# Scaling a retention read-out's rows on GpSimd, one multiplication per chunk, in a two-layer hybrid decoder trunk

## The chip, the cores and the metric

The kernel runs on one core of one Trainium2 chip. The metric is the time of one execution in microseconds on the device, the median of several runs; less is better. The profile calls the engines PE (TensorE, matmuls), PEld (its weight loads), DVE (VectorE), ACT (ScalarE), POOL (GpSimd) and SP (SyncE, which here only issues DMAs).

## The reference

Two layers over 512 positions of width 1024, in float32. Each layer normalizes x, projects it, sends the parts through three branches (an RWKV-7 recurrence, a chunked retention, a spatial gating unit), merges the three with sigmoid gates, and adds a gated MLP with a short convolution. The change touches the end of the retention branch:

```python
def retention_branch(p, cos, sin):
    ...
    y = (inner + cross).transpose(0, 2, 3, 1, 4).reshape(B, S, RET_HEADS, RET_V_DIM)
    y = y * lax.rsqrt(jnp.mean(y * y, axis=-1, keepdims=True) + EPS)
    return (y.reshape(B, S, RET_V_WIDTH) * jax.nn.silu(g)).astype(p.dtype)
...
        branches = jnp.stack([y_rw, y_ret, y_sg], axis=2)
        proj = jnp.einsum('bsgc,gcd->bsgd', branches, w_branch[l])
        gates = jax.nn.sigmoid(gate_logits.reshape(B, S, N_BRANCH, D_MODEL))
        x = x + jnp.sum(gates * proj, axis=2) @ w_out[l]
```

There are 4 heads of 128 columns, and 4 chunks of 128 positions. Each row of each head of y is divided by the root of its mean square.

## The kernel before, in words

**Matmuls and weights.** Every float32 product with weights is three matmuls (`mm3`, L153) over a high and a low half of both factors. A weight unit of 128x512 is loaded from HBM by SP into one of three raw buffers (`wr`, L123); ScalarE casts it to the high half (`sh` or `wh`, L136) and VectorE subtracts to get the low half (`sl` or `wl`, L137), after which the raw buffer may be loaded again. `unit` does this a few units ahead of the matmuls. Activations are split in the same way by `split` (L145 `hi` on ScalarE, L146 `lo` on VectorE). The products gather in PSUM accumulators: 4 of `acc`, 4 of `sm`.

**The order of the work.** The program is written in one sequence; a scheduler puts the instructions of every engine in an order, and `keep_in_program_order` pins some, the matmuls among them. Each engine then works off its own queue in that order. In the end of a layer's mixer the string `SEQ` sets the sequence: `0`, `1` and `2` are merges of one 128-column block with branch 0 (RWKV), 1 (retention) and 2 (spatial gating); `H` loads the retention's heads, `G` is a gating unit's output, and each `S` is one `ret_row`. The first `S` makes the scores, the second reads out chunks 0 and 1, the third chunks 2 and 3. `Y` is `ret_out`, which transposes the finished rows on TensorE (L964) and splits them for the merges `1`.

```python
SEQ = "0 H 0 0 0 G G S U U G S 0 G S 0 0 2 2 0 2 2 Y 2 1 2 1 2 1 2 1 1 1 1 1"
```

**The read-out.** For its two chunks `ret_row` squares the 8 head parts on ScalarE with a row sum each (L948), multiplies them from PSUM into the gate's tile on VectorE (L950, `yg`, which the profile calls `vt`), turns the sums into a mean plus epsilon (L951, `rss`), and lets GpSimd raise the 128x8 sums to the power -1/2 (L953, `rrr`). Each of the 8 parts of 128x128 is then scaled in place by its column of `rrr`, on ScalarE (L957).

**A merge** loads the gate from DRAM (L1027, `gth`), multiplies it with the accumulator on VectorE (L1028), which frees the accumulator, and adds to the running sum: on GpSimd for branch 2 (L1031), on VectorE for branch 1.

Of the kernel before, what the change touches and what calls it, by code (L numbers as in the profile page):

```python
# [10 lines left out]
AF = mybir.ActivationFunctionType  # L11
ALU = mybir.AluOpType
AX = mybir.AxisListType
ADD, SUB, MUL, POW, MAX = ALU.add, ALU.subtract, ALU.mult, ALU.pow, ALU.max
# [35 lines left out]
class Emit:  # L50
# [857 lines left out]
    def ret_row(self, read):  # L908


        nc, V, A, T, po = self.nc, self.nc.vector, self.nc.scalar, self.nc.tensor, self.tc.keep_in_program_order
        hv = [slice(0, 64), slice(64, 128)]
        X, new = [self.sm((128, 4, 128)) for _ in range(2)], [[True, True], [True, True]]
        hd = [(j, p, h) for j in range(2) for p in range(2) for h in (1, 0)]

        def mm(b, q, o, lhsT, rhs, stop=True):
            po(T.matmul(o, lhsT, rhs, start=new[b][q], stop=stop, skip_group_check=True))  # L917
            new[b][q] = False

        if read is None:  # L920
            for c in range(NC):
                for j, p, h in hd:
                    ts = slice(64 * p, 64 * p + 64)
                    mm(h, h ^ j, X[h][hv[h ^ j], c, ts], self.kF[j][hv[h], c, ts], self.qF[j][hv[h], c, ts])
            self.ret_states(0, 4)
            self.sc = [self.u((128, 8, 64), n="sc") for _ in range(2)]
            for h in range(2):
                V.tensor_tensor(self.sc[h], X[h].rearrange("q c (p t) -> q (c p) t", t=64), self.c("le64").unsqueeze(1).to_broadcast([128, 8, 64]), op=MUL)
            return
        cs = range(read, read + 2)  # L930
        for c in cs:
            for j, p, h in hd:
                i, o = 2 * j + h, h ^ j
                w = self.vt[c][hv[p], 128 * i:128 * i + 128] if p == o else self.vs[c][hv[o], j, :]
                mm(o, p, X[o][hv[p], 2 * (c - read) + j, :], self.sc[h][hv[o], 2 * c + p, :], w, c == p == 0)
        for c in cs:
            for j, p, h in hd:
                if c or p:
                    o, ts = h ^ j, slice(128 * c + 64 * p, 128 * c + 64 * p + 64)
                    q = self.qS if j else self.qF[0].rearrange("p c t -> p (c t)")  # L940
                    mm(o, p, X[o][hv[p], 2 * (c - read) + j, :], q[hv[o], ts], self.Rs[2 * c + p][hv[o], j, :])
        if read == 0:
            self.ret_states(4, 7)
        ss = self.small((128, 2, 4), "rss")
        for c in cs:
            sq, g = self.u((128, 4, 128), n="rsq"), self.yg[c]
            for i in range(4):
                A.activation(sq[:, i, :], X[i % 2 ^ i // 2][:, 2 * (c - read) + i // 2, :], AF.Square, accum_out=ss[:, c - read, i:i + 1])  # L948
            for o in range(2):
                V.tensor_tensor(self.heads(g, o), X[o][:, 2 * (c - read):2 * (c - read) + 2, :], self.heads(g, o), op=MUL)  # L950
        V.tensor_scalar(ss, ss, 4.0 / 128, 4e-6, op0=MUL, op1=ADD)  # L951
        rr = self.small((128, 2, 4), "rrr")
        nc.gpsimd.tensor_tensor(rr, ss, self.c("mhalf")[:, 0:8].rearrange("p (c i) -> p c i", i=4), op=POW)  # L953
        for c in cs:
            for i in range(4):
                o = self.yg[c][:, 128 * i:128 * i + 128]
                A.activation(o, o, AF.Copy, scale=rr[:, c - read, i:i + 1])  # L957

    def ret_out(self):
        out = []  # L960
# [344 lines left out]
```

## Time and profile before

| | |
|---|---|
| median of 3 runs | 1702.96 us (1702.8 to 1703.59) |
| profiled execution | 1703.05 us, of which the span of its instructions is 1701.3 us |
| granted TensorE clock | 0.999 |
| busy: PE, PEld, DVE, ACT, POOL | 1691.9, 1390.8, 1148.9, 766.5, 220.0 us |
| HBM | 181.92 MB read, 23.07 MB written, 120 GB/s over the span |

The read-outs lie near 388 to 408 us of the span in layer 0 and near 1234 to 1252 us in layer 1. A row of the time line reads: start, duration, engine, line, operation, output and inputs, shapes, count, and in brackets how long the engine had been idle and what ended that. A wait is put down to what came last. Idle time of an engine that nothing waits for costs nothing.

### The profile page before, as it was taken

What the parts mean: (1) busy time and instruction counts of PE and PEld (TensorE: products, weight loads), DVE (VectorE), ACT (ScalarE), POOL (GpSimd) and SP (SyncE); (2) the same over time, 40 slices, a digit from 0 to 9 for tenths busy, and PEclk for the clock granted to TensorE, in tenths of its full rate; (3) what the DMA queues carried; (4) which work ended last, traced back from release to release, by engine and by line L of the source; (5) the groups of instructions that cost most, each with busy time, mean ns of one, the idle gap of its engine ahead of it and who ended that gap; (6) DMA issues with size and microseconds to landing.
All of it is one profiled execution on the core that took longest, in us unless ns stands there. A gap on an engine that the chain in (4) does not pass through costs nothing.

```text
span 1701.3 us, 28310 instructions
## 1 busy us (share of the span) xinstructions
PE 1691.9 (99%) x10564; PEld 1390.8 (82%) x10564; DVE 1148.9 (68%) x2016; ACT 766.5 (45%) x1341; POOL 220.0 (13%) x274
## 2 busy tenths in 40 slices
PE   9999999999999999999999999999999999999998
PEld 7888877887888888888888888778888888888887
DVE  7887856567868777753358786565687788887432
ACT  7564433535445444342255634345354544444322
POOL 1122235102100000000011203341030000000010
PEclk9999999999999999999999999999999999999999
DMA  5335565446543333243332345555464444432531
GB/s 171 93 102 152 146 152 150 142 136 196 149 127 97 98 99 95 69 121 108 119 112 81 106 149 150 147 143 164 121 214 143 123 126 123 122 107 68 155 99 56
DMA packets 154409, 214.20 MB, mean 126 GB/s; under 512 B 48416, under 2 KB 57248, under 8 KB 154272
## 3 DMA queue, kind: packets, MB, share of 16 engines
q1 hardware_dynamic: 136464, 184.21, 36.6%
q10 hardware_dynamic: 12048, 19.00, 3.4%
q0 software_dynamic: 5760, 9.19, 2.6%
q8 instruction: 83, 1.36, 0.3%
q14 instruction: 54, 0.44, 0.1%
HBM read 181.92 MB, written 23.07 MB: 120 GB/s over the span
## 4 chain that ended last, share of the span: by engine, by line
PE 98%; DMA 1%; ACT 1%; DVE 0%; issue 0%; POOL 0%; SPq 0%; DVEq 0%; POOLq 0%; ACTq 0%
PE acc L153 87%; PE sm L153 4%; PE sm L649 2%; PE acc L289 1%; PE sm L563 1%; DMA wr<-wall 1%; PE sm L917 1%; PE acc L1014 0%; DMA x<-xT 0%; PE sm L900 0%; PE sm L526 0%; PE sm L525 0%; PE sm L807 0%; DVE sl L137 0%; PE sm L797 0%
## 5 line engine op out<-in xcount | busy, mean ns | idle before, releaser
L153 PE MATMUL acc<-lo,sh 128*128 128x512 f32 x1108 | 431.8, 390 | 1.1 <-DVE lo L146 0.8
L153 PE MATMUL acc<-hi,sh 128*128 128x512 f32 x1108 | 431.2, 389 | 0.0
L153 PE MATMUL acc<-hi,sl 128*128 128x512 f32 x1108 | 429.9, 389 | 0.0
L136 ACT CAST sh<-wr 128x512 fp32r<-128x512 f32 (+1 forms) x385 | 235.2, 616 | 382.4 <-PE acc L153 265.1
L137 DVE TENSOR_TENSOR sl<-wr,sh 128x512 fp32r<-128x512 f32 (+1 forms) x385 | 268.4, 700 | 143.4 <-ACT sh L136 82.0
L153 PEld LDWEIGHTS acc<-lo,sh 128*128 128x128 f32 x1108 | 207.9, 188 | 46.4 <-DVE lo L146 1.7
L153 PEld LDWEIGHTS acc<-hi,sl 128*128 128x128 f32 x1108 | 208.0, 188 | 43.5
L153 PEld LDWEIGHTS acc<-hi,sh 128*128 128x128 f32 x1108 | 208.0, 188 | 42.9 <-issue 0.2
L136 ACT CAST wh<-wr 128x512 fp32r<-128x512 f32 x194 | 120.2, 620 | 228.1 <-PE acc L153 204.7
L153 PE MATMUL acc<-lo,wh 128*128 128x512 f32 x556 | 219.5, 395 | 0.0
L153 PE MATMUL acc<-hi,wl 128*128 128x512 f32 x556 | 217.0, 390 | 0.0
L153 PE MATMUL acc<-hi,wh 128*128 128x512 f32 x556 | 216.6, 390 | 0.0
L137 DVE TENSOR_TENSOR wl<-wr,wh 128x512 fp32r<-128x512 f32 x195 | 139.1, 713 | 111.5 <-ACT wh L136 106.9
L153 PEld LDWEIGHTS acc<-lo,wh 128*128 128x128 f32 x556 | 104.3, 188 | 22.7 <-issue 0.3
L153 PEld LDWEIGHTS acc<-hi,wl 128*128 128x128 f32 x556 | 104.3, 188 | 22.6 <-issue 0.7
L153 PEld LDWEIGHTS acc<-hi,wh 128*128 128x128 f32 x556 | 104.4, 188 | 21.0
L153 PE MATMUL acc<-ah,sh 128*128 128x512 f32 x352 | 108.3, 389 | 0.0
L1081 DVE TENSOR_TENSOR fu<-acc,rsF 128x512 f32<-128x512 f32 x88 | 60.5, 690 | 70.3 <-PE acc L153 70.2
L1083 ACT ACTIVATE cv<-fu,pc 128x512 f32<-128x512 f32 x88 | 71.6, 816 | 46.9 <-DVE fu L1081 44.3
L1084 DVE SCALAR_TENSOR_TENSOR cv<-fu,pc,cv 128x511 f32<-128x511 f32 x88 | 65.5, 747 | 18.7 <-ACT cv L1083 18.7
L153 PE MATMUL acc<-wl,hi 128*128 128x512 f32 x192 | 78.0, 406 | 0.0
L153 PEld LDWEIGHTS acc<-ah,sh 128*128 128x128 f32 x352 | 66.1, 188 | 13.7
(334 smaller groups left out, 2420.9 us busy)
## 6 DMA issues: line engine op xcount, KB each, us to landing
wr<-wall SPq DMA_DIRECT2D x480, 256.0 KB, 2.7
gd<-gth ACTq DMA_DIRECT2D x48, 256.0 KB, 2.7
gth<-gd SPq DMA_DIRECT2D x48, 256.0 KB, 4.1
wr<-wdt SPq DMA_DIRECT2D x44, 256.0 KB, 2.8
wr<-wdn SPq DMA_DIRECT2D x40, 256.0 KB, 2.6
x<-xT SPq DMA_DIRECT2D x8, 256.0 KB, 4.8
tn<-ysq POOLq DMA_DIRECT2D x32, 64.0 KB, 3.3
tab<-rot ACTq DMA_DIRECT2D x8, 256.0 KB, 3.3
```

The lines of the kernel that those rows point to most:

```text
L136: self.kept((high or self.nc.scalar.copy)(hi[:, :n], raw[:, :n]))
L137: self.kept(self.nc.vector.tensor_tensor(lo[:, :n], raw[:, :n], hi[:, :n], op=SUB))
L153: i = self.nc.tensor.matmul(*x, **y, **kw)
L289: po(self.nc.tensor.matmul(pss[j], w[:, j * 128:j * 128 + 128], x, start=k == n == 0, stop=k == 7 and n == 2))
L563: i = T.matmul(pK[hv[1 - h], j, :], bk[hv[h], c, 1, :], x[hv[h], c, :], start=True, stop=True)
L649: po(T.matmul(o, l, r, start=start, stop=True, skip_group_check=True))
L917: po(T.matmul(o, lhsT, rhs, start=new[b][q], stop=stop, skip_group_check=True))
L1081: V.tensor_tensor(u, ps, self.rsF, op=MUL)
L1083: A.activation(t, u, AF.Identity, scale=self.p("cw2", j), bias=self.p("cb", j))
L1084: V.scalar_tensor_tensor(t[:, 1:], u[:, :511], self.p("cw1", j), t[:, 1:], op0=MUL, op1=ADD)
```

## The change

The 8 scalings of a read-out (4 heads in each of 2 chunks) leave ScalarE. GpSimd, which has just computed `rrr`, multiplies each chunk's whole 128x512 tile by the chunk's 4 columns of `rrr`, each repeated over the 128 columns of its head.

```diff
         nc.gpsimd.tensor_tensor(rr, ss, self.c("mhalf")[:, 0:8].rearrange("p (c i) -> p c i", i=4), op=POW)
         for c in cs:
-            for i in range(4):
-                o = self.yg[c][:, 128 * i:128 * i + 128]
-                A.activation(o, o, AF.Copy, scale=rr[:, c - read, i:i + 1])
+            o = self.yg[c].rearrange("p (i e) -> p i e", e=128)
+            nc.gpsimd.tensor_tensor(o, o, rr[:, c - read, :].unsqueeze(2).to_broadcast([128, 4, 128]), op=MUL)
```

The new multiplication is L956, and lines below it are one lower than before. GpSimd's queue in layer 0, from the first power to the first sums of the merges, before:

```order
L953 TENSOR_TENSOR rrr_4458<-rss_4442,con 128x8
L953 TENSOR_TENSOR rrr_4552<-rss_4536,con 128x8
L1031 TENSOR_TENSOR gth_4106<-gth_4106,gth_4606 128x512
L1031 TENSOR_TENSOR gth_4153<-gth_4153,gth_4629 128x512
L1031 TENSOR_TENSOR gth_4175<-gth_4175,gth_4674 128x512
```

and after, where vt_3732 and vt_3737 are the tiles of chunks 0 and 1, vt_3742 and vt_3747 those of chunks 2 and 3:

```order
L953 TENSOR_TENSOR rrr_4458<-rss_4442,con 128x8
L956 TENSOR_TENSOR vt_3732<-vt_3732,rrr_4458 128x512
L956 TENSOR_TENSOR vt_3737<-vt_3737,rrr_4458 128x512
L953 TENSOR_TENSOR rrr_4546<-rss_4530,con 128x8
L956 TENSOR_TENSOR vt_3742<-vt_3742,rrr_4546 128x512
L956 TENSOR_TENSOR vt_3747<-vt_3747,rrr_4546 128x512
L1030 TENSOR_TENSOR gth_4106<-gth_4106,gth_4594 128x512
```

Each power now has two multiplications behind it, and the sums of the merges stand behind the second pair. ScalarE's queue at the second read-out of layer 0, from its last squares to the first split of the transposed rows, before:

```order
L948 ACTIVATE rsq_4544,rss_4536<-sm_4502 128x128 x2
L136 CAST sh_4678<-wr_4631 128x512
L957 ACTIVATE vt_3742<-vt_3742,rrr_4552 128x128 x4
L957 ACTIVATE vt_3747<-vt_3747,rrr_4552 128x128 x4
L136 CAST sh_4701<-wr_4654 128x512
L136 CAST sh_4760<-wr_4676 128x512
L136 CAST sh_4783<-wr_4699 128x512
L136 CAST sh_4810<-wr_4758 128x512
L136 CAST sh_4833<-wr_4781 128x512
L136 CAST sh_4860<-wr_4808 128x512
L145 CAST hi_4725<-sm_4720 128x512
```

and after:

```order
L948 ACTIVATE rsq_4538,rss_4530<-sm_4496 128x128 x2
L136 CAST sh_4666<-wr_4619 128x512
L136 CAST sh_4689<-wr_4642 128x512
L136 CAST sh_4748<-wr_4664 128x512
L136 CAST sh_4771<-wr_4687 128x512
L136 CAST sh_4798<-wr_4746 128x512
L136 CAST sh_4821<-wr_4769 128x512
L136 CAST sh_4848<-wr_4796 128x512
L145 CAST hi_4713<-sm_4708 128x512
```

The scalings are gone from between the weight casts, and the rest keeps its order. TensorE's order is the same, row for row. On the other queues one weight cast with its low half moves one or two places ahead in layer 1, and one gate load of SP there stands one place later.

## The prediction

> **What bounds the kernel now.** I read the page first: its span, the busy shares and the chain of work that ended last.
>
> ```profile
> span 1701.3 us, 28310 instructions
> PE 1691.9 (99%) x10564; PEld 1390.8 (82%) x10564; DVE 1148.9 (68%) x2016; ACT 766.5 (45%) x1341; POOL 220.0 (13%) x274
> PE 98%; DMA 1%; ACT 1%; DVE 0%; issue 0%; POOL 0%; SPq 0%; DVEq 0%; POOLq 0%; ACTq 0%
> ```
>
> TensorE (PE) is busy for 1691.9 of 1701.3 us and is 98% of the chain. A busy matmul row is modelled, so a share alone does not say that nothing is lost between matmuls; the list of PE's waits (engine, line, whom it waited for, us in total, times, longest) and two stretches of the table of busy time by stage (span, then busy us of PE, weight loads, DVE, ACT, POOL) say how much there is to win.
>
> ```profile
> PE acc L310 <- DVE rst L307: 1.5, 1, 1.5
> PE acc L153 <- DVE lo L146: 0.8, 1, 0.8
> PE acc L289 <- ACT hi L213: 0.3, 1, 0.3
> PE acc L153 <- DVE gth L1028: 0.2, 1, 0.2
> 395.00:405.00 10.00, 9.73 (x42) 7.45 (x41) 7.75 (x15) 5.89 (x23) 0.78 (x1) 1.00 0.61 192
> 415.00:425.00 10.00, 9.17 (x41) 7.26 (x40) 7.69 (x12) 4.68 (x9) 4.48 (x3) 1.00 0.78 241
> ```
>
> Everything that PE waits for comes to 2.8 us (1.5 + 0.8 + 0.3 + 0.2). The first and the third wait belong to the kernel's start. The second and the fourth, 1.0 us together, lie in layer 0 in the two stretches above, that is around the retention read-outs that the change touches. Layer 1 has no wait of PE at all. So this change can win about 1.0 us through work done earlier, and it can lose only if it makes PE wait where it does not today.
>
> **What is removed: 32 scalings on ScalarE.** The rows of the scaling's line and of the power ahead of it (engine, operation, count, then shortest, median and longest ns), each with a line on waiting:
>
> ```profile
> L957 ACT ACTIVATE vt<-vt,rrr x32: 386/388/405, 392.4 to 1251.2; 128x128 f32<-128x128 f32 x32
>   POOL rrr L953: 5.9, 4
> L953 POOL TENSOR_TENSOR rrr<-rss,con x4: 1643/1644/1952, 390.8 to 1247.1; 128x8 f32<-128x8 f32 x4
> ```
>
> They stand in four groups of 8 (two read-outs in each of two layers). Added up they are 32 x 0.388 = 12.4 us; they overlap a little, and a group takes 2.45 us from its first start to its last end. Ahead of them ScalarE stands still for the power in GpSimd, 5.9 us in four waits. The change frees about 4 x 2.45 + 5.9 = 15.7 us of an engine that is busy 45% of the span: worth nothing by itself. What it is worth is what waits behind it. Layer 0, in order of time (start, us, engine, line, and in brackets the idle time before with its cause):
>
> ```profile
> 389.86 0.22 ACT L948 ACTIVATION_READ_ACCUMULATOR rsq<-sm 128x1 f32 x1
> 392.43 2.45 ACT L957 ACTIVATE vt<-vt,rrr 128x128 f32<-128x128 f32 x8 [2.36 <-POOL rrr L953]
> 395.42 0.69 DVE L137 TENSOR_TENSOR sl<-wr,sh 128x512 fp32r<-128x512 f32 x1 [2.98 <-ACT sh L136]
> 403.99 0.68 DVE L1028 SCALAR_TENSOR_TENSOR gth<-gth,acc 128x512 f32<-128x512 f32 x1
> 404.72 0.50 PE L153 MATMUL acc<-lo,sh 128*128 128x512 f32 x1 [0.21 <-DVE gth L1028]
> 403.42 0.64 ACT L136 CAST sh<-wr 128x512 fp32r<-128x512 f32 x1
> 405.79 0.69 DVE L1028 SCALAR_TENSOR_TENSOR gth<-gth,acc 128x512 f32<-128x512 f32 x1 [0.52 <-DMA gth<-gd]
> 405.90 2.45 ACT L957 ACTIVATE vt<-vt,rrr 128x128 f32<-128x128 f32 x8 [1.84 <-POOL rrr L953]
> 408.26 1.13 ACT L136 CAST sh<-wr 128x512 fp32r<-128x512 f32 x2
> 408.90 0.69 DVE L137 TENSOR_TENSOR sl<-wr,sh 128x512 fp32r<-128x512 f32 x1 [2.42 <-ACT sh L136]
> 410.10 0.69 DVE L137 TENSOR_TENSOR sl<-wr,sh 128x512 fp32r<-128x512 f32 x1
> 416.42 0.62 ACT L136 CAST sh<-wr 128x512 fp32r<-128x512 f32 x1 [1.08 <-DMA wr<-wall]
> 416.95 2.04 ACT L145 CAST hi<-sm 128x512 fp32r<-128x512 f32 x4
> 418.57 0.50 PE L153 MATMUL acc<-lo,sh 128*128 128x512 f32 x1 [0.83 <-DVE lo L146]
> ```
>
> Both groups hold back weight casts (L136) that stand behind them in ScalarE's order. VectorE therefore idles 2.98 and 2.42 us until it can make the low halves (L137). An L137 also gives a raw weight buffer back, so SP issues the next weight load later; the cast at 416.42 waits 1.08 us for such a load, the cast of the transposed retention rows stands behind it until 416.95, and PE waits 0.83 us for their low half. The 0.21 us at 404.72 is an accumulator that VectorE frees late, for the same lag. Without the scalings the casts can go at about 390.1 and 404.1, where the squares' last row (389.86 + 0.22) and the cast behind the second squares (403.42 + 0.64) end: the second lot 4.2 us before 408.26.
>
> **What is added: 8 multiplications of 128x512 on GpSimd.** No row has this operation with an operand repeated along the row, so I bound it by the rows that exist (count, busy us, mean ns, then idle time before):
>
> ```profile
> L1031 POOL TENSOR_TENSOR gth<-gth,gth 128x512 f32<-128x512 f32 x16 | 24.9, 1564 | 38.4 <-DVE gth L1028 38.4
> L1144 POOL TENSOR_TENSOR ya<-ya,fg 128x512 f32<-128x512 f32 x4 | 5.5, 1377 | 0.3
> ```
>
> The low end is 1.3 us, the shortest sum (the row of 1251.05 below); the high end is twice the mean sum, 2 x 1.56 = 3.1 us, in case repetition costs a second pass. I take 1.4 us, near L1144, which is a multiplication of the same shape. The chain to the transposes is the power and two multiplications, in one queue, and these rows say how much room it has:
>
> ```profile
> 404.22 1.64 POOL L953 TENSOR_TENSOR rrr<-rss,con 128x8 f32<-128x8 f32 x1 [11.83 <-DVE rss L951]
> 410.27 3.38 POOL L1031 TENSOR_TENSOR gth<-gth,gth 128x512 f32<-128x512 f32 x2 [4.40 <-DVE gth L1028]
> 413.10 1.91 PE L964 MATMUL sm<-con,vt 128*128 128x128 f32 x16
> 1247.12 1.95 POOL L953 TENSOR_TENSOR rrr<-rss,con 128x8 f32<-128x8 f32 x1 [8.48 <-DVE rss L951]
> 1251.05 1.29 POOL L1031 TENSOR_TENSOR gth<-gth,gth 128x512 f32<-128x512 f32 x1 [1.97 <-DVE gth L1028]
> 1257.19 1.91 PE L964 MATMUL sm<-con,vt 128*128 128x128 f32 x16
> ```
>
> Layer 0: the power ends at 405.86, the rows are ready at 405.9 + 2.8 = 408.7, and PE reads them at 413.10: 4.4 us to spare. Layer 1: 1249.07 + 2.8 = 1251.9 against 1257.19: 5.3 us. The first read-out's rows have longer: in layer 0 from 392.43 to 413.10, 20.7 us. Behind the multiplications in GpSimd's queue stand only the sums of the merges (L1031). The first of them in layer 0 starts at 410.27 and loses nothing; in layer 1 it moves from 1251.05 to 1251.9, and since the 16 sums have 38.4 us of idle time ahead of them (the L1031 row), a delay of 0.9 us is caught up. Cost on the path: nothing, with 4.4 us of cover. PE's order is the same, row for row; no DMA is added or removed.
>
> **VectorE beside GpSimd.** A VectorE instruction with both inputs in SBUF stops while GpSimd works, one that reads an accumulator does not:
>
> ```profile
> 410.71 0.68 DVE L1028 SCALAR_TENSOR_TENSOR gth<-gth,acc 128x512 f32<-128x512 f32 x1
> 411.30 1.19 DVE L137 TENSOR_TENSOR sl<-wr,sh 128x512 fp32r<-128x512 f32 x1
> 430.71 1.29 POOL L1031 TENSOR_TENSOR gth<-gth,gth 128x512 f32<-128x512 f32 x1 [3.03 <-DVE gth L1028]
> 430.72 1.83 DVE L146 TENSOR_TENSOR lo<-gth,hi 128x512 fp32r<-128x512 f32 x1
> ```
>
> The L146 that starts 0.01 us behind a sum ends at 432.55, 0.55 us after the sum's end at 432.00: it waited the sum out, then ran. L1028 beside a sum keeps its 0.68 us. The Trainium skill, "SBUF — State Buffer", section "SBUF: two separate sides", describes this as an exclusive lock that is held for a whole instruction while the other engine is blocked; the rows agree with it. By that rule the change pays for ScalarE's free time with stalls of VectorE, and the sum stays as it is here, because these rows price the stalls already.
>
> In my sum a pair of multiplications holds off one or two L137, at most 2 x 1.4 = 2.8 us, in places where VectorE idles 2.98 and 2.42 us today. Step by step in the second group of layer 0: the L137 of 408.90 may start at about 406.5, waits for the first multiplication to end at 407.3, ends at 407.9 instead of 409.6 (1.7 us sooner); the next one, behind an L1028, waits for the second multiplication to end at about 409.1 and ends at 409.7 instead of 410.8 (1.1 us sooner). 1.1 us covers the 0.83 us that PE loses at 418.57, and ScalarE's earlier squares cover the 0.21 us.
>
> The sum: -0.83 - 0.21 = -1.04 us, nothing added. The profiled execution took 1703.05 us (1701.3 of span and 1.75 around it), 0.09 above the median of the three runs, 1702.96. Forecast: 1703.05 - 1.04 - 0.09 = 1701.9 us.
>
> **Rivals.** Changes within 0.2% (3.4 us) can't be told from none by a measurement of this kernel.
>
> First, nothing is won: the stalls of VectorE by GpSimd eat the lead, or the loads from HBM arrive no sooner, and PE's 0.83 us stay: 1703.0 us. Layer 1 can then lose a little, since its first transposed rows are ready just in time:
>
> ```profile
> 1260.01 2.47 DVE L146 TENSOR_TENSOR lo<-sm,hi 128x512 fp32r<-128x512 f32 x4
> 1261.67 0.39 PE L153 MATMUL acc<-lo,sh 128*128 128x512 f32 x1
> ```
>
> Four halves take 2.47 us, the first is ready at about 1260.7, and PE needs it at 1261.67: 1.0 us of cover. One multiplication's length (1.4) more would cost 0.4 us: 1703.4. With two groups of that kind it is 1703.8.
>
> Second, slower, by GpSimd alone: the operand repeated along the row makes a multiplication so long that the transposes wait. The points are (413.10 - 405.86) / 2 = 3.6 us in layer 0 and (1257.19 - 1249.07) / 2 = 4.1 us in layer 1. At 5 us each it is 2 x 1.4 + 2 x 0.9 = 4.6 us: 1707.6. For it speaks only that no row shows the operation; against it, that even the high end, 3.1 us, lies below the point.
>
> Third, slower by the stall of VectorE: if all 8 multiplications reached PE one for one through VectorE, 8 x 1.4 = 11.2 us, 1714. It decides wherever VectorE's lead over PE is under 1.4 us; the rows above show one such place (1.0 us), and elsewhere VectorE idles when the multiplications come. The lock in the Trainium skill's page is the rule that speaks for this one.
>
> Fourth, the freed time counts in full: 15.7 us: 1703.0 - 15.7 = 1687.3. Against it stands that PE waits only 1.0 us in these places.
>
> **How the numbers follow.** The forecast has 60%, nothing won (or a little lost in layer 1) 33%, the long multiplication 3%, the stall of VectorE in full 2%, the full gain 2%. The first two lie within 0.2%: same 93%, slower 5%, faster 2%. The likeliest case alone spans 1701.4 to 1702.4 (half a microsecond to either side, since only part of the 0.83 may go, or PE's start after a wait is quicker too). The range reaches from 1701.1, somewhat under it, to 1704.0, the end of the first rival.
>
> **What the changed profile would show.** No ACT row of the scaling; 8 POOL rows of 1.3 to 1.7 us, the last pair ended before 409.5 in layer 0; idle time before L137 near 395 and 409 gone or below 1 us, with one or two L137 near 407 stretched beyond 1.1 us; PE's waits for lo (0.8) and gth (0.2) gone; transposes that wait for nothing. Wrong it would be with a multiplication above 3.6 us, with a wait of PE on GpSimd, or with a new wait of PE for lo in layer 1.

## The result, and the profile after

| | before | after |
|---|---|---|
| median (22 runs each) | 1702.84 us | 1700.57 us (1700.22 to 1703.28) |
| profiled execution, its span | 1703.05, 1701.3 us | 1700.23, 1698.5 us |
| ACT busy, instructions | 766.5 us, 1341 | 757.4 us, 1309 |
| POOL busy, instructions | 220.0 us, 274 | 230.2 us, 282 |

The ratio is 0.9987, 95% interval 0.9982 to 0.9993: 2.3 us less. The forecast was 1701.9 us, 1.0 us less, so the direction was right and the gain more than twice the size; 1700.57 lies 0.5 us below the range. From the page of the changed kernel: span, busy time, the chain of work that ended last.

```profile
span 1698.5 us, 28286 instructions
PE 1689.8 (99%) x10564; PEld 1390.7 (82%) x10564; DVE 1150.2 (68%) x2016; ACT 757.4 (45%) x1309; POOL 230.2 (14%) x282
PE 99%; DMA 0%; ACT 0%; DVE 0%; issue 0%
```

PE's waits (engine, line, whom it waited for, us in total, times, longest), and the two stretches of the table of busy time in which PE waited before:

```profile
PE acc L310 <- DVE rst L307: 1.5, 1, 1.5
PE acc L289 <- DVE wh L136: 0.9, 1, 0.9
395.00:405.00 10.00, 10.00 (x46) 8.28 (x45) 7.78 (x16) 5.69 (x22) 4.03 (x3) 1.00 0.83 281
415.00:425.00 10.00, 10.00 (x45) 8.28 (x45) 5.96 (x9) 3.11 (x5) 3.17 (x2) 1.00 0.48 161
```

Both waits that are left belong to the kernel's start. In the two stretches PE is busy throughout and has 46 and 45 matmul rows where it had 42 and 41. That is eight more, and at the usual distance between two starts (0.227 us, below) eight are 1.8 us: already more than the 1.0 us of waits that the list of before shows.

GpSimd in layer 0, in order of time (start, us, engine, line, shapes, count, idle time before with its cause), then all its multiplications in one row (shortest, median and longest ns, first and last start):

```profile
391.91 2.91 POOL L956 TENSOR_TENSOR vt<-vt,rrr 128x512 f32<-128x512 f32 x2
400.90 1.64 POOL L953 TENSOR_TENSOR rrr<-rss,con 128x8 f32<-128x8 f32 x1 [6.08 <-DVE rss L951]
402.62 2.42 POOL L956 TENSOR_TENSOR vt<-vt,rrr 128x512 f32<-128x512 f32 x2
405.02 2.97 POOL L1030 TENSOR_TENSOR gth<-gth,gth 128x512 f32<-128x512 f32 x2
```
```profile
L956 POOL TENSOR_TENSOR vt<-vt,rrr x8: 1036/1442/1547, 391.9 to 1247.8; 128x512 f32<-128x512 f32 x8
```

A multiplication takes 1.44 us. The second power now starts at 400.90, 3.3 us sooner than before: the freed first group moves all that follows. The rows of chunks 2 and 3 are ready at 405.04. ScalarE, VectorE and the transposes in the same stretch:

```profile
389.64 1.66 ACT L136 CAST sh<-wr 128x512 fp32r<-128x512 f32 x3
391.79 0.68 DVE L137 TENSOR_TENSOR sl<-wr,sh 128x512 fp32r<-128x512 f32 x1
393.05 2.32 DVE L137 TENSOR_TENSOR sl<-wr,sh 128x512 fp32r<-128x512 f32 x2
406.95 1.58 DVE L137 TENSOR_TENSOR sl<-wr,sh 128x512 fp32r<-128x512 f32 x1 [0.77 <-ACT sh L136]
411.71 1.47 PE L963 MATMUL sm<-con,vt 128*128 128x128 f32 x12
412.34 2.06 ACT L145 CAST hi<-sm 128x512 fp32r<-128x512 f32 x4
413.11 2.48 DVE L146 TENSOR_TENSOR lo<-sm,hi 128x512 fp32r<-128x512 f32 x4
```

The weight casts follow the squares without a gap (389.64); the transposes wait for nothing; the split of the transposed rows begins at 412.34 instead of 416.95. VectorE pays beside the first pair of multiplications: two L137 take 2.32 us, which take 1.29 where nothing is scaled (e4 below). Another L137 takes 1.58 us, but beside the second sum of a merge; the kernel before has such rows too (411.30, in the prediction).

Why 1.0 us of listed waits were worth more shows in PE's rows of the kernel before, around its three losses in layer 0 (start, us):

```profile
400.37 0.39 PE L153 MATMUL acc<-hi,sl 128*128 128x512 f32 x1
400.81 0.50 PE L153 MATMUL acc<-lo,sh 128*128 128x512 f32 x1
401.15 0.39 PE L153 MATMUL acc<-hi,sh 128*128 128x512 f32 x1
...
404.12 0.39 PE L153 MATMUL acc<-hi,sl 128*128 128x512 f32 x1
...
405.06 0.40 PE L153 MATMUL acc<-hi,sh 128*128 128x512 f32 x1
...
417.35 0.39 PE L153 MATMUL acc<-hi,sl 128*128 128x512 f32 x1
...
418.90 0.39 PE L153 MATMUL acc<-hi,sh 128*128 128x512 f32 x1
```

Undisturbed, starts stand 0.227 us apart (404.12 follows 403.89), though a row is drawn 0.39 us long: rows overlap by 0.16 us. A gap is listed as idle only from the end of the row, so each wait is listed 0.16 us short. And the matmul after a gap runs 0.50 us, with the next start 0.335 us behind it: 0.11 us more. From start to start the loss is

- at 400.81: 0.44 - 0.227 + 0.11 = 0.32 us, with no wait listed at all (the row before ends at 400.76);
- at 404.72: 0.60 - 0.227 + 0.11 = 0.48 us, listed as 0.21;
- at 418.57: 1.22 - 0.227 + 0.11 = 1.10 us, listed as 0.83;

together 1.90 us. By comparing the start of the same matmul in both traces, the changed kernel gains 2.06 us in layer 0 from 390 us to 420 us of the kernel before (417.6 of the changed one). The remaining 0.7 us of the two spans' difference (2.8) is 0.5 ahead of that, at the start, and 0.3 near 911 us and behind it, where the two kernels are the same; when the changed kernel ran again (e1 below) these two were 0.2 and 0.1, so they vary from execution to execution. Nothing is gained at layer 1's read-outs. The Trainium skill, "Perfetto Trace Analysis", section "Tensor Engine Instruction (MATMUL, LD_WEIGHTS)", says that a matmul's end is an estimate; rows that overlap by 0.16 us on one engine agree with it.

### The profile page after: what moved, and what is told of

Read it like the earlier page. It is cut to its first block, busy times and chain, and to the rows that moved or that the text cites. A ratio compares the mean times of both kernels' runs of the same rounds, so it can differ in the third digit from the quotient of the medians.

```text
span 1698.5 us, 28286 instructions
## 1 busy us (share of the span) xinstructions
PE 1689.8 (99%) x10564; PEld 1390.7 (82%) x10564; DVE 1150.2 (68%) x2016; ACT 757.4 (45%) x1309; POOL 230.2 (14%) x282
## 4 chain that ended last, share of the span: by engine, by line
PE 99%; DMA 0%; ACT 0%; DVE 0%; issue 0%
PE acc L153 88%; PE sm L153 4%; PE sm L649 2%; PE acc L289 1%; PE sm L563 1%; PE sm L917 1%; PE acc L1013 0%; PE sm L900 0%; DMA g<-pcols 0%; PE sm L526 0%; PE sm L525 0%; PE sm L963 0%; PE sm L807 0%; PE sm L797 0%; PE sm L580 0%; PE sm L581 0%
## 5 line engine op out<-in xcount | busy, mean ns | idle before, releaser
L137 DVE TENSOR_TENSOR sl<-wr,sh 128x512 fp32r<-128x512 f32 (+1 forms) x385 | 269.4, 703 | 136.5 <-ACT sh L136 73.6
L137 DVE TENSOR_TENSOR wl<-wr,wh 128x512 fp32r<-128x512 f32 x195 | 139.4, 715 | 111.1 <-ACT wh L136 107.1
```

Of the source, the lines that this page charges most:

```text
L137: self.kept(self.nc.vector.tensor_tensor(lo[:, :n], raw[:, :n], hi[:, :n], op=SUB))
```

## Experiments

An inserted line moves the line numbers below it by one to five: L1028 of before may read L1030 here, and so on. TensorE's waits at the kernel's start are left out below.

**The change again, one layer alone, and no scaling at all.** "e2" and "e3" let GpSimd scale in one layer and ScalarE in the other:

```diff
+            if self.layer == 0:      # 1 in the second
+                (GpSimd's multiplication)
+                continue
+            (ScalarE's four scalings)
```

"e4" leaves the scaling out, and with it both the work of ScalarE and the multiplications of GpSimd (written here against the changed kernel):

```diff
-        for c in cs:
-            o = self.yg[c].rearrange("p (i e) -> p i e", e=128)
-            nc.gpsimd.tensor_tensor(o, o, rr[:, c - read, :].unsqueeze(2).to_broadcast([128, 4, 128]), op=MUL)
```

> The changed kernel itself, for comparison on the same chip. Theory A: the gain is three places in layer 0 (near 400, 404 and 417 us of the span before) where TensorE lost start-to-start time, 0.32 + 0.48 + 1.10 = 1.9 us with the slow matmul behind each; so 1.6 to 2.4 us less than before. Theory B: 1.0 us of it is what the listed waits show, and the rest is not the read-out's (the start of the kernel, or the order moved in layer 1).

> GpSimd scales the rows in layer 0 alone; layer 1 keeps ScalarE. Theory A: the whole gain of the changed kernel, 1.6 to 2.4 us, and no listed wait of TensorE behind the start. Theory B: about 1.0 us.

> GpSimd scales the rows in layer 1 alone; layer 0 keeps ScalarE. Theory A: no change (within 0.4 us), with the waits of 0.8 and 0.2 us of TensorE still in layer 0. Theory B: about 1.0 us less than before.

> The scaling of the retention rows is left out, on any engine (the power is still computed). If GpSimd's multiplications cost something through VectorE's stalls, this is faster than the changed kernel by up to 1 us. Theory A: TensorE waits for nothing in either, so the two agree within 0.4 us, 1.6 to 2.4 us under the kernel before.

| kernel (before: 1702.52) | us | ratio, 95% |
|---|---|---|
| e1, the change again | 1700.57 | 0.9987 [0.9979, 0.9996] |
| e2, layer 0 alone | 1700.63 | 0.9990 [0.9981, 0.9999] |
| e3, layer 1 alone | 1702.81 | 1.0002 [0.9993, 1.0011] |
| e4, no scaling | 1700.44 | 0.9988 [0.9979, 0.9997] |

PE's waits behind the start: none in e1, e2 and e4; in e3 those of layer 0 are back.

```profile
PE acc L153 <- DVE lo L146: 1.2, 1, 1.2
PE acc L153 <- DVE gth L1033: 0.4, 1, 0.4
```

The whole gain is made in layer 0. Leaving the multiplications out as well gives nothing further (1700.44 beside 1700.57), so VectorE's stalls beside GpSimd, 1.0 us in the row at 393.05 alone, cost the kernel nothing.

**Which read-out, and the wait or the work.** "e5" gives GpSimd only the read-out of chunks 0 and 1 (`read == 0`), "e6" only that of chunks 2 and 3. "e7" keeps the changed kernel and puts on ScalarE only the wait for the power, by a copy of one column into a new small tile; "e8" puts there only the work, 8 scalings of scratch data by a constant:

```diff
# e7, behind GpSimd's multiplications
+        A.activation(self.small((128, 1), "aw"), rr[:, 0, 0:1], AF.Copy)
# e8, ahead of the power; sqs holds the tiles of squares
+        for i in range(8):
+            A.activation(sqs[0][:, i % 4, :], sqs[1][:, 3, :], AF.Copy, scale=2.0)
```

> GpSimd scales the first read-out's rows (chunks 0 and 1) in both layers, ScalarE the second's. Theory A: the losses near 400 and 404 us go (0.32 + 0.48 = 0.8 us less), the one near 417 stays if it hangs on the second group of scalings: TensorE still waits 0.5 to 0.8 us for the low half. Rival: the lag is one and the same, handed on from the first group, and all 1.9 us go.

> GpSimd scales the second read-out's rows alone, ScalarE the first's. Theory A: the loss near 417 us goes (1.1 us less), the small waits near 400 and 404 stay. Rival: nothing goes, since the lag comes from the first group.

> The changed kernel, and where ScalarE scaled it now does one 128x1 copy of the power's result: it waits for GpSimd's power as before, but scales nothing. Layer 0's casts are held about 2 us per read-out, not 4.5. Theory A (any hold ahead of the casts counts, and 1.1 us of lead are enough): 1.2 to 2.2 us less than before. Rival (the wait is the cause): no gain.

> The changed kernel, and where ScalarE scaled it now does 8 scalings of 128x128 on a scratch tile that need no power: the work of 2.45 us per read-out without the wait. Theory A: as with the wait alone, 1.2 to 2.2 us less than before. Rival (the work is the cause): no gain.

| kernel (before: 1702.62) | us | ratio, 95% |
|---|---|---|
| e5, chunks 0 and 1 | 1700.31 | 0.9985 [0.9976, 0.9994] |
| e6, chunks 2 and 3 | 1701.59 | 0.9993 [0.9984, 1.0002] |
| e7, wait, new tile | 1708.33 | 1.0032 [1.0019, 1.0045] |
| e8, work | 1700.63 | 0.9987 [0.9978, 0.9996] |

e5 has no wait of PE behind the start; e6 has two small ones:

```profile
PE acc L153 <- DVE gth L1032: 0.3, 1, 0.3
PE acc L153 <- DVE lo L146: 0.2, 1, 0.2
```

Freeing the first read-out brings everything, though the waits of the list lay behind the second: a lag made near 392 us is handed on. Freeing the second alone gives a time between the two, though its interval reaches no change; from start to start it still loses time at 404.1 and 417.2, though the second read-out is freed. The work alone costs nothing, but it was less than intended: scaled by a constant, the 8 took 1.71 us and not 2.45. e7 told nothing on its own question: it lost 8 us with no wait of PE in the read-outs, and its matmuls were slower in stretches far away.

**More work on GpSimd, and VectorE in its place.** "e9", "e10" and "e11" put 1, 2 and 4 further multiplications of each chunk, into scratch, ahead of the real one, "e12" gives the multiplication to VectorE:

```diff
+            for _ in range(1):       # 2 in e10, 4 in e11
+                nc.gpsimd.tensor_tensor(sqs[c - read], o, rr[:, c - read, :].unsqueeze(2).to_broadcast([128, 4, 128]), op=MUL)
# e12
-            nc.gpsimd.tensor_tensor(o, o, rr[:, c - read, :].unsqueeze(2).to_broadcast([128, 4, 128]), op=MUL)
+            V.tensor_tensor(o, o, rr[:, c - read, :].unsqueeze(2).to_broadcast([128, 4, 128]), op=MUL)
```

> The changed kernel with one more multiplication of the same kind into a scratch tile ahead of each: 4 instead of 2 per read-out, 5.8 us by the 1.44 us that one took. In layer 0 the last rows are ready at 402.6 + 5.8 = 408.4 against the transposes at 411.7: as the changed kernel, within 0.5 us. If VectorE's stalls count, slower by up to 2 us.

> Two more ahead of each: 6 per read-out, 8.6 us, ready at 411.3 against 411.7 in layer 0, and at 1246.3 + 8.6 = 1254.9 against 1254.4 in layer 1: the edge of the cover. Within 1 us of the changed kernel; more if VectorE's stalls add up or the sums of the merges, which now start 6 us later, hold something.

> Four more ahead of each: 10 per read-out, 14.4 us, beyond the cover by 402.6 + 14.4 - 411.7 = 5.3 us in layer 0 and 6.3 in layer 1. The order of the matmuls also moves by some rows here. Expected: TensorE waits on GpSimd at the transposes, 5 to 12 us slower than the changed kernel. If it is within 2 us, the transposes are not what the rows are needed for.

> VectorE does the 8 multiplications, not GpSimd: the wait for the power then stands in VectorE's queue ahead of the low halves and of the products that free accumulators. Expected: the waits of TensorE come back, 0 to 2 us slower than the kernel before. If only ScalarE's queue matters: as the changed kernel.

| kernel (before: 1702.73) | us | ratio, 95% |
|---|---|---|
| e9, twice | 1700.65 | 0.9988 [0.9979, 0.9998] |
| e10, three times | 1709.07 | 1.0037 [1.0023, 1.0050] |
| e11, five times | 1720.80 | 1.0106 [1.0089, 1.0123] |
| e12, VectorE | 1701.01 | 0.9987 [0.9978, 0.9997] |

e9 and e12 have no wait of PE behind the start. In e10 (the first row below) and e11 (the second) PE waits for GpSimd's rows:

```profile
PE sm L966 <- POOL vt L959: 5.0, 3, 2.0
```
```profile
PE sm L966 <- POOL vt L959: 10.8, 2, 5.8
```

GpSimd in e10 at the second read-out of layer 0, and 10 us of the table of busy time in layer 1 (the last three figures are the granted clock, the DMA share and GB/s):

```profile
403.61 1.64 POOL L954 TENSOR_TENSOR rrr<-rss,con 128x8 f32<-128x8 f32 x1 [2.74 <-DVE rss L952]
411.61 1.72 POOL L1033 TENSOR_TENSOR gth<-gth,gth 128x512 f32<-128x512 f32 x1
413.29 1.49 POOL L959 TENSOR_TENSOR vt<-vt,rrr 128x512 f32<-128x512 f32 x1
1260.00:1270.00 10.00, 8.51 (x37) 7.12 (x38) 4.64 (x8) 2.77 (x5) 6.88 (x6) 0.83 0.43 134
```

So 2 x 1.44 = 2.9 us for a chunk leave the transposes alone, and 3 x 1.44 = 4.3 us do not. But in e10 it is not the length alone: the second power came at 403.61, 2.7 us later than in the changed kernel, because VectorE's stalls now delay the read-out itself, and a sum of a merge got in ahead of the last multiplication. Without these two the rows would have been ready at about 411.3, just ahead of the transposes at 411.7. e10 also lost more than the sum of its waits (5.5 us): 8.5 us beside the changed kernel. In part each wait is listed too short, as above; in part the matmuls behind the waits of layer 1 were slow. The granted clock there is 0.83, and from 1264.03 to 1265.73 they start 0.43 us apart, which makes 1.3 us in all. The five executions go from 1706.81 us (mean clock 0.999) to 1711.18 (0.996). e11 has mean clock 0.995 in all of its four, with 0.68 from 420 to 430 us, behind a wait of 5.8 us, and a few of its matmuls stand in another order, so its size shows only the direction. The waits that e12 was expected to bring back did not come: VectorE does a multiplication in 0.69 us and has that time here. So what matters here is that ScalarE is rid of the scaling, and not which of the two other engines gets it.

**The wait and the work together, and the loss of e7.** "e15" is the changed kernel, with 8 scratch scalings on ScalarE that use the power's result as ScalarE's scalings did before: wait and work, but off the data path. "e13" is e7 with a new tile of 64 bytes a row in place of 4. "e14" is the changed kernel with nothing but a new tile of 4 bytes a row (in two buffers), set once at the start and never used:

```diff
# e15
+        for i in range(8):
+            A.activation(sqs[0][:, i % 4, :], sqs[1][:, 3, :], AF.Copy, scale=rr[:, i // 4, i % 4:i % 4 + 1])
# e13
+        A.activation(self.small((128, 16), "aw")[:, 0:1], rr[:, 0, 0:1], AF.Copy)
# e14
         V.memset(self.rst, 1.0)
+        V.memset(self.small((128, 1), "aw"), 0.0)
```

> The run with the wait alone, with the copy's small tile made 64 bytes a row, not 4. In the first form TensorE waited for nothing at the read-outs, but its matmuls came up to 2% slower in stretches far from them. If the 4-byte tile's shift of the buffers behind it is what did that, this run has the changed kernel's matmul pace (531 matmuls in 1560 to 1680 us) and, since the wait alone holds the casts about 2 us, its time: within 0.4 us of it. If the wait itself costs, it is 1 us or more slower than the changed kernel.

> The changed kernel with a 128x1 tile (4 bytes a row, two buffers) added to the small tiles and written once at the start; nothing reads it. If shifted buffers slow TensorE, 5 to 8 us slower than the changed kernel, with about 519 matmuls in 1560 to 1680 us. If not, the same as the changed kernel.

> GpSimd scales the rows, and ScalarE also does 8 scalings by the power on a scratch tile where it did them before: wait and work together, about 4.5 us per read-out ahead of the casts, while no row hangs on it. Theory A (the sum of the hold counts, since wait and work alone are each within the lead): 1.0 to 2.1 us of the gain go again, and TensorE's waits for gth and lo in layer 0 return. If the gain came from the rows being ready earlier, this is as fast as the changed kernel.

Measured beside 1702.79 before: e13 1713.79 (1.0064 [1.0051, 1.0076]), e14 1708.55 (1.0033 [1.0021, 1.0045]), e15 1702.85 (1.0000 [0.9991, 1.0009]). e15 loses the gain, and PE's waits are back, somewhat longer than before the change:

```profile
PE acc L153 <- DVE lo L146: 1.2, 1, 1.2
PE acc L153 <- DVE gth L1030: 0.4, 1, 0.4
```

e14 answers for e7: without any wait on ScalarE it loses as much. PE waits nowhere behind the start, the granted clock is 1.00, and still matmuls start further apart; one stretch long after the read-outs, in the changed kernel and then in e14:

```profile
1560.00:1680.00 120.00, 120.00 (x531) 99.37 (x530) 46.06 (x68) 34.89 (x61) 7.24 (x8) 1.00 0.34 102
```
```profile
1560.00:1680.00 120.00, 120.00 (x518) 97.13 (x518) 50.12 (x73) 37.80 (x66) 7.26 (x8) 1.00 0.34 106
```

**The same with no buffer moved, and other moves.** "e16" repeats e7's wait, written into a tile of squares that is done with, so that no tile is added. "e17" adds e14's instruction at the start without its tile. "e18" is e14 with 256 bytes a row in two buffers, so that what lies behind moves by 512 bytes:

```diff
# e16
+        A.activation(sqs[1][:, 3, 0:1], rr[:, 0, 0:1], AF.Copy)
# e17
+        V.memset(self.rst[:, 0:1], 1.0)
# e18
+        V.memset(self.small((128, 64), "aw"), 0.0)
```

> The wait alone, as in the run with a 128x1 copy of the power's result on ScalarE, but written into the first column of a tile of squares that is no longer needed: no buffer is added and none moves. GpSimd scales. If what that earlier run lost came from the moved buffers and not from the wait, this runs like the changed kernel: 1700.6 us, no wait of TensorE in the read-outs. If the wait for the power alone costs time in the read-outs, waits for lo come back there and it is at 1701.5 to 1702.8. If the wait costs 8 us in some hidden way, it is at 1708.

> The changed kernel with one more memset of one column of an existing tile at the start, and no tile added: the control for the run that added an 8-byte tile. If moved buffers made that one slow, this is at 1700.6 us with 529 to 533 matmuls between 1560 and 1680 us. If the extra VectorE instruction at the start did it, 1708.5 with about 518.

> The changed kernel with an unused tile of 128x64 (two buffers, 512 bytes of every row) set once at the start; every small tile made later, and the pools behind them, move by 512 bytes. If any move of these buffers slows TensorE, 1707 to 1714 us. If only the position within 512 bytes matters, as 8 and 128 bytes both were slow, it is at 1700.6 with 531 matmuls between 1560 and 1680 us. If the moved buffers can also come to lie better, it is below 1700.

| kernel (before: 1701.98) | us | ratio, 95% |
|---|---|---|
| e16, wait alone | 1700.43 | 0.9992 [0.9982, 1.0001] |
| e17, instruction alone | 1700.46 | 0.9990 [0.9981, 1.0000] |
| e18, moved by 512 bytes | 1700.16 | 0.9988 [0.9978, 0.9997] |

All three run like the changed kernel, with 531 matmuls in the stretch shown and no wait of PE behind the start, though the intervals of e16 and e17 reach no change. Their read-outs are alike all the same. Matmul by matmul, from 390 to 420 us of the kernel before, the gain is 2.06 us in e1, e2, e4, e5, e8, e9, e16, e17 and e18, 1.85 in e12 and 1.00 in e6, while e3 and e15 lose 0.6 and 0.4 us there. So e7, e13 and e14 lost time by where buffers lay, as far as these runs tell; the traces show no addresses. ScalarE in e16, and then in e15, at the same places (the copy or the scalings, the casts behind them, the split):

```profile
391.27 0.20 ACT L958 ACTIVATE rsq<-rrr 128x1 f32<-128x1 f32 x1 [2.36 <-POOL rrr L954]
391.38 1.64 ACT L136 CAST sh<-wr 128x512 fp32r<-128x512 f32 x3
412.79 2.04 ACT L145 CAST hi<-sm 128x512 fp32r<-128x512 f32 x4
```
```profile
391.92 2.45 ACT L959 ACTIVATE rsq<-rsq,rrr 128x128 f32<-128x128 f32 x8 [2.36 <-POOL rrr L954]
394.28 1.65 ACT L136 CAST sh<-wr 128x512 fp32r<-128x512 f32 x3
416.42 2.04 ACT L145 CAST hi<-sm 128x512 fp32r<-128x512 f32 x4
```

Executions differ by some tenths in when they reach the read-out, so the hold is counted from the start of the last square. The casts follow it by 0.52 us in the changed kernel, by 2.02 in e8, 2.84 in e16 and 5.10 in e15 (5.09 before the change). Work alone holds them back by 1.5 us and the wait by 2.3, and both are free; wait and work hold them back by 4.6 us, and that costs the whole gain.

What PE waits for at the end is the low half of the transposed rows (L146). Its rows in the kernel before, in e6 and in e3, the last with the L137 ahead of it:

```profile
417.83 2.47 DVE L146 TENSOR_TENSOR lo<-sm,hi 128x512 fp32r<-128x512 f32 x4
```
```profile
416.51 2.47 DVE L146 TENSOR_TENSOR lo<-sm,hi 128x512 fp32r<-128x512 f32 x4
```
```profile
416.03 1.84 DVE L137 TENSOR_TENSOR sl<-wr,sh 128x512 fp32r<-128x512 f32 x1 [0.52 <-ACT sh L136]
417.79 2.47 DVE L146 TENSOR_TENSOR lo<-sm,hi 128x512 fp32r<-128x512 f32 x4
```

Its start orders the runs: from 413.1 to 414.8 (after, e2, e8, e16, e5) PE loses nothing for it, at 416.5 (e6) it waits 0.2 us, at 417.8 to 417.9 (before, e3, e15) 0.8 to 1.2 us. The split on ScalarE alone does not order them: in e3 it starts at 415.90, 1.05 us sooner than before, but an L137 beside a sum of GpSimd keeps VectorE until 417.8.

## Why the prediction was right and wrong

- **The bound and the place: right.** PE stays at 99% of the chain, only the read-outs of layer 0 had something to win, and both waits there are gone. e2 and e3 show the place.
- **The size of the gain: wrong.** The step that failed is the sum's first term, "-0.83 - 0.21 = -1.04 us". It took the idle times of the list of waits for the loss. From start to start these two waits were worth 1.10 + 0.48 us, and a third gap of 0.32 us stood in no list, since it was about as short as the overlap of two rows: 1.90 us, against 2.3 us (interval 1.2 to 3.1) between the medians. With the smaller steps between matmuls the read-outs were worth 2.06 us. The mechanism of the gain was right, and the term was mis-sized. The "everything that PE waits for" ahead of it has the same flaw, and the range's low end, with half a microsecond for "PE's start after a wait", was too near for it.
- **Which lag does it: only half right.** The prediction worked the gain out at the second group (1.7 and 1.1 us sooner). e5 shows that freeing the first group is enough; e6 shows that with the second alone freed half of the loss stays (1.00 of 2.06 us gained), so the lag of the first lot of weights arrives at the second. With both freed the whole stretch moved, and the split came 4.6 us sooner.
- **GpSimd's price: right.** 1.44 us against the 1.4 taken. The rows were ready at 405.04, not at 408.7, for the earlier power; the transposes had 6.7 us to spare, not 4.4. The second rival's point of 3.6 us was not measured: e9 (2.9 us) lies below it and e10 (4.3 us) above it, but e10 waits for other reasons too, and with the earlier power the point itself moved to (411.71 - 402.54) / 2 = 4.6 us.
- **The stall of VectorE: seen, and free.** The L137 rows of 2.32 us are there, e4 shows that they cost nothing, and e10 that stalls count once GpSimd has three times the work, through the later power. So the third rival had the stall right and its cost wrong.
- **Nothing won: refuted.** e1, e2, e5, e8, e9, e12 and the changed kernel itself have intervals that exclude it. The chances had this and the forecast in one class, within 0.2%, and the ratio of 0.9987 is in it.
- **The freed time in full (15.7 us): refuted.** Only the part of a hold beyond the slack counted, and the slack lies between 2.3 and 4.6 us.

## What to carry to other kernels

Where matmuls run back to back, price a stall from start to start of the same engine's rows, less the usual distance, plus the slow restart; the list of waits leaves out the overlap of the rows, and all of a gap no longer than that. A held-up engine cost nothing here up to its slack, and the place to free it was the first hold in the chain, not the one in front of the listed wait that was the longest. An arm of an experiment that adds a tile needs a control that adds the tile alone.

## What the runs showed of the hardware

The place of buffers within a row of SBUF changed the pace of TensorE. A new tile of 2 x 4 bytes a row that is never used (e14) cost 8.0 us beside the changed kernel's 1700.57, one of 2 x 64 bytes (e13) about 13, one of 2 x 256 bytes (e18) nothing; the instructions stand in the same order in e14 and e18. In e14's stretch of 120 us the table has 518 matmul rows for 531: starts 0.232 us apart for 0.227, at clock 1.00, with no wait listed. Three sizes fit a rule by which the position within 512 bytes counts, but do not prove one. Which operand it is, and whether a better place than the present one exists, was not tried.

A stall of TensorE can cost more than its own length. In e10 a single transpose stood between two waits of 1.99 and 1.11 us in layer 1, and the granted clock was 0.83 over the 10 us in which they ended; around the one wait of 1.93 us in layer 0 it stayed at 1.00. In e11 it was 0.68 over the 10 us in which a wait of 5.8 us ended.
